# The second score product of both attentions: 64 rows of the array, or all 128

## The chip, the cores and the metric

The kernel runs as one program on one core of a Trainium2 chip. The metric is device time in microseconds (us) of one execution; lower is better. The core has a tensor engine (PE in the profile; its weight loads are listed apart, as PEld), a vector engine (DVE), a scalar engine (ACT), GpSimd (POOL), and DMA queues issued mostly from SyncE (SP).

## The reference

Two transformer blocks in a row, on 512 tokens of width 1024, in float32. Cut to what matters here:

```
# block 1: mixer = banded attention + pooling, gated; then a gated feed-forward with a short convolution
sc = einsum('bqhd,bkhd->bhqk', q_c, k_c) * scale + bias      # 8 heads of 64 features
p  = softmax(sc);  y = einsum('bhqk,bkhd->bqhd', p, v_c)

# block 2: gated delta rule (4 heads of 128) + differential attention (4 heads of 2 x 64)
sc = einsum("bqhcd,bkhcd->bhcqk", q_i, k) * scale            # c = 0, 1: two score maps for a head
p  = softmax(where(mask, sc, -inf));  p = p[:, :, 0] - lam * p[:, :, 1]
o  = einsum("bhqk,bkhe->bqhe", p, v)
```

In both attentions a score is a sum over 64 features, and causality leaves 128, 256, 384 or 512 keys for the four blocks of 128 queries.

## The kernel before

**Exactness.** Large products are made in float32r from operands that are split in two: a high part (the value copied to float32r) and a low part (what the copy lost, by a subtraction on the vector engine). A product is three passes: high by high, high by low, low by high. Each is a weight load of 128 columns and a matmul of up to 512 columns.

**Scores.** A score contracts over 64 features, half of the array's 128 rows. `stack_q` makes, for each of two heads (`j` = 0, 1), a tile of 128 partitions: the head's own 64 partitions hold the high part of the queries and the other 64 their low part. `stack_k` makes for each head a tile with the high part of the keys in both halves (`ka`, `kb`), and one tile `kl` with the low parts of both heads, each in its own half. `score` then needs two matmuls: the first over all 128 rows gives (q_hi + q_lo) k_hi, the second over the head's own 64 rows gives q_hi k_lo. The queries are the weights of both, the keys stream.

**Where they run.** Block 1 has 8 heads with 4 query blocks each: 32 scores (`attn_item`), their tiles stacked from an SBUF tile in `evac_qk`, once for each of four head pairs. Block 2 has 4 heads with 4 query blocks and 2 maps: 32 scores (`diff_item`), their tiles stacked from a PSUM bank in `to_heads`, once for each of four heads. So `stack_k` is called eight times and `score` 64 times.

**Order.** Each engine works through its instructions in the order in which they were issued. The class `Issue` keeps estimated times for every engine and tile; attention, convolution, delta rule and norms are background tasks (generators) which `step()` lets go on between two matmuls of the large products, when by these estimates their inputs are there. `Engine` wraps every engine, so that every instruction stands under one line (L230) in the profile. The estimate for a matmul does not depend on its rows:

```
            m, exact = ins[0].free_size(), ins[0].dtype != F32R
            t = (4 * max(n, m) if exact else max(n, m / 2) + 240 * self.exact) / 2400 + 0.003
```

**Buffers.** Tiles of 128 x 512 (`act(...)`) come from one pool of 75 buffers. Scores use two PSUM banks (`s`), transposes and small products three (`t`), large products three (`mm`). The weight stream (`w32`, `whi`, `wlo`) is fetched on the SP queue and split on ACT and DVE while the large products run.

**What consumes the result.** In block 1 the attention output (`ah`, `al`) is needed by the branch product that follows the gates. In block 2 the last product takes the heads in the order `HEADS`: the first six of them in all output tiles, then the last two, whose weights wait in tiles `wk`. Heads 6 and 7 are heads of the differential attention (`oh`, `ol`).

Of the kernel before, what the change touches and what calls it, by code (L numbers as in the profile page):

```python
# [29 lines left out]
# block 2's projections in order: a and z are feature-major tiles, the others two heads token-major  # L30
UNITS = ["a6", "a10", "a4", "a1", "a8", "a7", "a3", "a5", "a2", "a9", "q1", "v0", "a0", "q0",
         "k0", "z5", "a11", "k1", "z3", "z0", "z2", "z4", "z1", "z6", "z7", "v1"]
# heads in the order in which the last product takes them: the first of them in all tiles, then the others
# [7 lines left out]
# issue order: a task goes on when its last results are LEAD us away, unless an engine has SLACK us of work  # L41
# [23 lines left out]
def weight_order():  # L65
    """(array, piece, first column, end) in the order of use"""
    o = []

    def add(name, i=None, a=0, b=None):
        o.append((name, i, a, b))  # L70

    for hp in range(4):
        add("w_qk", 2 * hp)
        add("w_qk", 2 * hp + 1)
        if hp == 0:
            for i in range(4):
                add("w_v", i)
    add("w_pg")
    for i in range(4):
        add("w_u", i)  # L80
    for m in range(KD):
        add("w_g", 2 * m)
        add("w_g", 2 * m + 1)
        add("w_ap", m)
    for m in range(KD):
        add("w_o", m)
    for i in range(2 * MF):
        add("w_up", i)
    for m in range(KD):
        for a, b in ((0, 8), (8, 15), (15, 22)):  # L90
            add("w_dn", m, a * P, b * P)
    for u in UNITS:
        if u[0] in "az":
            add("w2_" + u[0], int(u[1:]))
        else:
            add("w2_" + u, 0)
            add("w2_" + u, 1)
    for m in range(KD):
        add("w_out", m)
    return o  # L100
# [5 lines left out]
class Issue:  # L106
    """Order of issue. Each engine works through its instructions in the order in which they are issued;
    the times that are kept here, in us, are estimates and decide that order alone."""
# [45 lines left out]
    def issue(self, e, op, outs, ins, func=None):  # L154
        self.count += 1
        lat = {"PE": 0.2, "V": 0.13, "A": 0.13, "G": 0.13}[e]
        start = max(self.free[e], self.ready(*ins) + lat)
        if e == "PE":
            start = max(start, self.now)
        # one engine at a time works on a PSUM bank  # L160
        held = [self.bank.setdefault(x.name, {}) for x in (*outs, *ins) if x.space == PSUM]
        for d in held:
            start = max([start] + [t + 0.05 for o, t in d.items() if o != e])
        if func in TABLES and TABLES[func] != self.table:
            self.table = TABLES[func]
            start += 1.28
        t = start + self.cost(e, op, outs, ins)
        for d in held:
            d[e] = t
        self.free[e] = t  # L170
        if e == "PE":
            self.now = t
        self.done(outs, t + (0.05 if e == "PE" else 0.0))
# [16 lines left out]
    def step(self):  # L190
        """tasks whose results have come go on; between two yields a task's work is issued together"""
        for task in list(self.tasks):
            if task[0] > self.now + LEAD:
                continue
            if not task[2] and max(self.free["V"], self.free["A"]) > self.now + SLACK:
                continue
            self.mark = task[3]
            r = next(task[1], "end")
            if r == "end":
                self.tasks.remove(task)  # L200
            else:
                task[0], task[3] = self.now if r == 0 else self.mark, self.mark
# [13 lines left out]
class Engine:  # L216
    """An engine whose instructions are counted by an Issue."""
# [18 lines left out]
def kernel(ctx, tc, aps, out, dbg=None):  # L236
# [13 lines left out]
    # PSUM banks: of each kind the time at which a bank's last readers are done  # L250
# [21 lines left out]
    # ---- background tasks: generators; "yield" waits for what was just issued, "yield 0" does not  # L272
# [4 lines left out]
    def move(dst, src):  # L277
        """a transfer within the chip's memories"""
# [3 lines left out]
    def grab_all(tag, n):  # L282
        """PSUM banks whose last readers are done"""
# [70 lines left out]
    # ---- weight stream: fetched three pieces ahead, split two ahead  # L354
# [16 lines left out]
    def split_next():  # L371
# [11 lines left out]
        elif key[0] == "w_out" and key[1] < NPART:  # L383
            # the first heads' weights pass through, the others' stay
# [26 lines left out]
    def weights(*key):  # L411
        """the next piece of the stream"""
        w = take(*key)
        advance()
        return w
# [6 lines left out]
    def wcol(w, k):  # L422
        """the weights of one k, of a piece that may wait in two halves"""
        return w[k // 4][:, k % 4 * P:(k % 4 + 1) * P] if isinstance(w, list) else w[:, k * P:(k + 1) * P]

    def mm(ps, w, x, start, stop):
        """a slice of a large product; while its operands are on their way other work goes on"""
# [34 lines left out]
    def copy(dst, src, scale=None):  # L462
        """on the engine that is free first"""
# [7 lines left out]
    def scale_rows(t, r):  # L471
        """t[p, c] *= r[p, c]"""
# [21 lines left out]
    def rstd(acc, col, tbs):  # L494
        """col[token] = 1 / rms and the same spread over the partitions"""
# [10 lines left out]
    class Seam:  # L506
        """x += rms_norm(f) and the next operand x * g split in two parts, one half of the tokens at a
        time: the norm of the first half runs under the products of the second."""
# [61 lines left out]
    def project_norm(wkeys, hi, lo, gname, seam, gnext):  # L570
        """f = W^T act in 8 output tiles; wkeys(m) lists each tile's pieces and their k ranges"""
# [27 lines left out]
    # ------------------------------------------------------------------ block 1: mixer  # L599
    # the first two products begin while their operands arrive  # L600
# [16 lines left out]
    # the tensor engine's clock rises while it works  # L617
# [60 lines left out]
    def attn_item(h, qb):  # L678
        """scores and softmax of (head, 128 queries)"""
# [40 lines left out]
    def attn_values():  # L720
        """transposed probabilities times values, (head pair, 128 keys) at a time"""
# [46 lines left out]
    def stack_q(src):  # L768
        """two heads of 64 features: for each its high part and, in the other half of the partitions, its low part"""
# [9 lines left out]
    def stack_k(src):  # L779
        """for each of two heads its high part in both halves, and their low parts"""  # L780
        a, b, lo = act("ka", F32R), act("kb", F32R), act("kl", F32R)
        parts = ((a, LOW, HIGH), (b, HIGH, LOW))
        for t, own, other in parts:
# [3 lines left out]
        for t, own, _ in parts:  # L787
            V.tensor_tensor(lo[own], src[own], t[own].bitcast(F32), op=ALU.subtract)
        return a, b, lo

    def score(ps, q, k, j, qs, n):
        """(q_hi + q_lo) k_hi, then q_hi k_lo"""
        own = (LOW, HIGH)[j]
        T.matmul(ps, q[j][:, qs], k[j][:, :n], start=True, stop=False)
        T.matmul(ps, q[j][own, qs], k[2][own, :n], start=False, stop=True)
# [56 lines left out]
    # pooling branch  # L852
# [44 lines left out]
    # gates, branch outputs, their mix  # L897
# [45 lines left out]
    # ------------------------------------------------------------------ block 1: feed-forward  # L943
# [37 lines left out]
    def seam_products(sn, keys, finish):  # L981
        """the first products after a seam, one half of the tokens at a time"""
# [72 lines left out]
    # inverses of the blocks of 16 x 16 go into zeros  # L1055
# [11 lines left out]
    # ------------------------------------------------------------------ block 2  # L1067
# [8 lines left out]
    def delta_gates():  # L1076
        """decays and write strengths, column c * 4 + h"""
# [74 lines left out]
    def gdn_pair(hs):  # L1152
        """two heads of the delta rule; chunks of 128 tokens. k, q and v carry a factor 2 from silu."""
# [12 lines left out]
        def decays():  # L1166
            """the chunks' running log decays on all partitions"""
# [41 lines left out]
        # the diagonal blocks of 64 x 64 of the chunks: [128, NT, 64], rows 0-63 one block, rows 64-127 the other  # L1209
        BLOCKS = ((LOW, LOW), (HIGH, HIGH))  # L1210
        halves = lambda t: t[:, :256].rearrange("p (c d) -> p c d", c=NT)
        # L passes through DRAM, where its diagonal blocks of 16, 32 and 64 lie at even distances
# [3 lines left out]
        def diag(t, n, row, w):  # L1216
            """of each of the diagonal blocks of n x n the rows from row on and w columns: [chunk, block, row, column]"""
# [38 lines left out]
        # off the inverse's path: values, keys and attention weights of the chunks  # L1256
# [46 lines left out]
        # inverse of I + L: 16 x 16 diagonal blocks by substitution, one block to a partition, then three merges  # L1303
# [31 lines left out]
        def inverse(i):  # L1335
            # T: transposed inverse of the blocks, D: the inverse, both compact
# [107 lines left out]
    def finish_head(o, ssq, idx, eps, nq=None):  # L1444
        """rms norm over the head, weight, silu(z), split: o is token-major [128, NT, 128]"""
# [29 lines left out]
    def tok_unit(nm, half_):  # L1475
        """token-major projection of two heads (256 columns): two [128, 2, 256] tiles of token blocks"""
# [26 lines left out]
    def v_unit():  # L1503
        """token-major values of the first two heads with the delta rule's b and a"""
# [21 lines left out]
    def rope_norm(nm, tok_):  # L1526
        """rms norm over 64 (its factor returned for q, applied for k) and rotation, in place"""
# [122 lines left out]
    # the residual waits in DRAM until the last product  # L1650
# [38 lines left out]
    def out_part(ps, w, a, b, cs=FULL, start=True, stop=True):  # L1689
        """the heads in places a to b"""  # L1690
# [20 lines left out]
    # the first heads in all tiles, then the last heads; three tiles wait in PSUM, the others' sums go to the residual  # L1711
# [29 lines left out]
def _pack(inputs):  # L1741
# [4 lines left out]
    def tiles(w):  # L1746
        """[K, N] -> [N/128, 128, K] pieces: one output tile's weights, k tiles side by side."""
# [3 lines left out]
    def tok_pieces(w, n):  # L1751
        """[1024, m*n] -> [m, 2, 128, 4*n]: token-major operands, half of k in each piece."""
# [94 lines left out]
```

## Time and profile before

| | us |
|---|---|
| median of 3 runs | 1041.13 |
| lowest and highest run | 1040.13, 1042.51 |
| span of the profiled execution | 1042.7 |
| PE busy in it | 1024.7 (98%) |
| PE weight loads busy | 849.2 (81%) |
| DVE busy | 684.9 (66%) |
| ACT busy | 499.5 (48%) |

The profiled execution is another one than the three timed; the page gives its span, from the first to the last instruction, and no time around it. Busy shares are means over the whole span. A matmul's end is modelled, so the durations of neighbouring matmuls overlap and PE looks busy also where it is not at its peak; what a matmul costs in a row of others is read from start to start. The granted TensorE clock is given as a share of its upper level, 2.4 GHz.

### The profile page before, as it was taken

Reading aid. Unit: us, or ns where it says so; the run is one execution under the profiler, and the core shown is the slowest. Engines: PE = TensorE matmul, PEld = TensorE weight load, DVE = VectorE, ACT = ScalarE, POOL = GpSimd, SP = SyncE. Lnnn points to the kernel's source line nnn. Section 1 sums busy time; section 2 is a strip of 40 time slices with the busy share of each in tenths; the row PEclk is TensorE's granted clock in tenths of the full one; section 3 lists DMA queues with packets and bytes.
Section 4 is the critical chain, followed back from the end, with each engine's and each line's share of the span. In section 5 each row is a group of like instructions: output and inputs, shape, how many; then the busy total and the mean of one; then the engine's idle time right before and its main releaser. Section 6 shows DMA issues by size and latency. Waiting matters only on the chain. (4 is left out here: it accounts for less than half of the span.)

```text
span 1042.7 us, 15097 instructions
## 1 busy us (share of the span) xinstructions
PE 1024.7 (98%) x5718; PEld 849.2 (81%) x5718; DVE 684.9 (66%) x1409; ACT 499.5 (48%) x1039; POOL 74.5 (7%) x146
## 2 busy tenths in 40 slices
PE   8999999999999999999999999999999989999998
PEld 7966678888888888888888888898899978887876
DVE  6576774444447897766776522359885687997873
ACT  6566643333244554434434421334456674667670
POOL 3000000000002200000001000004100450001001
PEclk9999999999999999999999999999999998999999
DMA  7321122332332133233233323330533530023212
GB/s 261 133 71 49 63 70 92 102 96 88 100 110 73 61 102 101 82 100 101 90 94 116 102 85 112 91 122 8 177 102 107 143 92 22 21 62 122 70 53 81
DMA packets 40345, 97.19 MB, mean 93 GB/s; under 512 B 12160, under 2 KB 16528, under 8 KB 40272
## 3 DMA queue, kind: packets, MB, share of 16 engines
q1 hardware_dynamic: 37392, 87.53, 26.7%
q0 software_dynamic: 2736, 8.66, 2.4%
q8 instruction: 45, 0.74, 0.3%
q14 instruction: 28, 0.23, 0.1%
q10 hardware_dynamic: 144, 0.03, 0.0%
HBM read 90.29 MB, written 5.91 MB: 92 GB/s over the span
## 5 line engine op out<-in xcount | busy, mean ns | idle before, releaser
L230 DVE TENSOR_TENSOR wlo<-w,whi 128x1024 fp32r<-128x1024 f32 (+4 forms) x153 | 180.5, 1185 | 63.7 <-ACT whi L230 63.7
L230 PE MATMUL mm<-nh,whi 128*128 128x512 f32 x448 | 177.5, 396 | 0.0
L230 PE MATMUL mm<-nl,whi 128*128 128x512 f32 x448 | 177.4, 396 | 0.0
L230 PE MATMUL mm<-nh,wlo 128*128 128x512 f32 x448 | 177.2, 395 | 0.0
L230 ACT ACTIVATE whi<-w 128x1024 fp32r<-128x1024 f32 (+4 forms) x153 | 154.9, 1017 | 40.3 <-DMA w<-w_dn 22.0
L230 PEld LDWEIGHTS mm<-nh,whi 128*128 128x128 f32 x448 | 84.3, 188 | 18.5 <-issue 0.8
L230 PEld LDWEIGHTS mm<-nh,wlo 128*128 128x128 f32 x448 | 84.3, 188 | 18.3 <-issue 0.2
L230 PEld LDWEIGHTS mm<-nl,whi 128*128 128x128 f32 x448 | 84.3, 188 | 18.0 <-issue 0.2
L230 PE MATMUL mm<-h,whi 128*128 128x512 f32 x208 | 83.5, 402 | 0.0
L230 PE MATMUL mm<-h,wlo 128*128 128x512 f32 x208 | 83.3, 400 | 0.0
L230 PE MATMUL mm<-l,whi 128*128 128x512 f32 x208 | 83.2, 400 | 0.0
L230 PE MATMUL mm<-gh,whi 128*128 128x512 f32 (+1 forms) x198 | 73.0, 369 | 0.0
L230 PE MATMUL mm<-gh,wlo 128*128 128x512 f32 (+1 forms) x198 | 72.8, 368 | 0.0
L230 PE MATMUL mm<-gl,whi 128*128 128x512 f32 (+1 forms) x198 | 72.8, 368 | 0.0
L230 ACT ACTIVATE y<-hu,par 128x512 f32<-128x512 f32 x40 | 32.6, 814 | 65.6 <-DVE hu L230 65.6
L230 DVE SCALAR_TENSOR_TENSOR y<-hu,par,y 128x511 f32<-128x511 f32 x80 | 59.8, 748 | 1.4
L230 POOL TENSOR_TENSOR acc<-acc,sq 128x256 f32<-128x256 f32 (+1 forms) x31 | 26.2, 846 | 426.0 <-ACT sq L230 425.9
L230 DVE TENSOR_TENSOR hu<-mm,nb 128x512 f32<-128x512 f32 x40 | 27.6, 690 | 42.2 <-PE mm L230 42.2
L230 PE MATMUL mm<-wlo,nh 128*128 128x256 f32 (+1 forms) x192 | 55.3, 288 | 0.0
L230 PE MATMUL mm<-whi,nl 128*128 128x256 f32 (+1 forms) x192 | 55.0, 287 | 0.0
L230 PE MATMUL mm<-whi,nh 128*128 128x256 f32 (+1 forms) x192 | 55.0, 286 | 0.0
L230 DVE TENSOR_TENSOR acc<-acc,sq 128x512 f32<-128x512 f32 (+1 forms) x21 | 14.3, 682 | 49.9 <-ACT sq L230 49.8
(343 smaller groups left out, 2203.2 us busy)
## 6 DMA issues: line engine op xcount, KB each, us to landing
w<-w_up SPq DMA_DIRECT2D x44, 512.0 KB, 3.5
w<-w_g SPq DMA_DIRECT2D x16, 512.0 KB, 3.5
w<-w_dn SPq DMA_DIRECT2D x16, 448.0 KB, 3.4
w<-w_a SPq DMA_DIRECT2D x12, 512.0 KB, 3.5
w<-w_ap SPq DMA_DIRECT2D x8, 512.0 KB, 3.5
w<-w_o SPq DMA_DIRECT2D x8, 512.0 KB, 3.4
w<-w_dn SPq DMA_DIRECT2D x8, 512.0 KB, 3.6
w<-w_z SPq DMA_DIRECT2D x8, 512.0 KB, 3.8
```

The lines of the kernel that those rows point to most:

```text
L230: return f(*args, **kw)
```

## The change

`stack_k` now makes four tiles: `ka` and `kb` as before, and `la` and `lb`, which hold a head's low part of the keys in both partition halves. `score`'s second matmul takes all 128 rows of the query tile and of `la` or `lb`. It computes (q_hi + q_lo) k_lo: the term q_lo k_lo, left out before, comes in. For each call of `stack_k` there are four subtractions on DVE in the place of two, and four buffers in the place of three. Numbers and sizes of matmuls stay. The rest of the diff takes out comments and docstrings.

```
     def stack_k(src):
-        a, b, lo = act("ka", F32R), act("kb", F32R), act("kl", F32R)
-        parts = ((a, LOW, HIGH), (b, HIGH, LOW))
-        for t, own, other in parts:
+        a, b, la, lb = act("ka", F32R), act("kb", F32R), act("la", F32R), act("lb", F32R)
+        parts = ((a, la, LOW, HIGH), (b, lb, HIGH, LOW))
+        for t, _, own, other in parts:
             A.activation(t[own], src[own], AF.Copy)
             A.activation(t[other], src[own], AF.Copy)
         yield
-        for t, own, _ in parts:
+        for t, lo, own, other in parts:
             V.tensor_tensor(lo[own], src[own], t[own].bitcast(F32), op=ALU.subtract)
-        return a, b, lo
+            V.tensor_tensor(lo[other], src[own], t[own].bitcast(F32), op=ALU.subtract)
+        return a, b, la, lb
 
     def score(ps, q, k, j, qs, n):
-        own = (LOW, HIGH)[j]
         T.matmul(ps, q[j][:, qs], k[j][:, :n], start=True, stop=False)
-        T.matmul(ps, q[j][own, qs], k[2][own, :n], start=False, stop=True)
+        T.matmul(ps, q[j][:, qs], k[2 + j][:, :n], start=False, stop=True)
```

## Rows read from the trace of the kernel before

**Rows 1.** The page, part 1: busy us, share of the span, instructions.
```profile
PE 1024.7 (98%) x5718; PEld 849.2 (81%) x5718; DVE 684.9 (66%) x1409; ACT 499.5 (48%) x1039; POOL 74.5 (7%) x146
```

**Rows 2.** Busy time by stretch: from:to, length, engines (instructions), clock, DMA share, GB/s.
```profile
44.00:122.00 78.00, 78.00 (x343) 49.89 (x341) 52.74 (x152) 48.77 (x118) 1.61 (x3) 1.00 0.19 65
880.00:946.00 66.00, 65.11 (x431) 53.21 (x430) 61.03 (x190) 44.45 (x136) 0.00 (x0) 1.00 0.15 47
946.00:1020.00 74.00, 73.90 (x415) 59.95 (x414) 57.10 (x190) 51.46 (x151) 4.31 (x8) 1.00 0.25 79
```

**Rows 3.** Timeline of PE, block 1: start us, duration us, instruction, rows*columns, operand.
```profile
118.65 0.34 PE L230 MATMUL s<-kb,qb 128*128 128x384 f32 x1
118.92 0.43 PE L230 MATMUL s<-kl,qb 64*128 64x384 f32 x1
119.29 0.50 PE L230 MATMUL s<-kb,qb 128*128 128x512 f32 x1
119.72 0.50 PE L230 MATMUL s<-kl,qb 64*128 64x512 f32 x1
120.15 0.50 PE L230 MATMUL mm<-l,whi 128*128 128x512 f32 x1
120.48 0.40 PE L230 MATMUL mm<-h,wlo 128*128 128x512 f32 x1
120.72 0.39 PE L230 MATMUL mm<-h,whi 128*128 128x512 f32 x1
```

**Rows 4.** Timeline of the weight loads (PEld) of the same stretch.
```profile
118.42 0.19 PEld L230 LDWEIGHTS s<-kb,qb 128*128 128x128 f32 x1
118.92 0.18 PEld L230 LDWEIGHTS s<-kl,qb 64*128 64x128 f32 x1 [0.31 <-issue]
```

**Rows 5.** Timeline of PE, block 1, a score over 256 keys.
```profile
52.54 0.28 PE L230 MATMUL s<-kb,qb 128*128 128x256 f32 x1
52.75 0.38 PE L230 MATMUL s<-kl,qb 64*128 64x256 f32 x1
53.06 0.50 PE L230 MATMUL mm<-l,whi 128*128 128x512 f32 x1
53.40 0.40 PE L230 MATMUL mm<-h,wlo 128*128 128x512 f32 x1
```

**Rows 6.** Timeline of PE, block 2, two scores over 128 keys.
```profile
927.89 0.22 PE L230 MATMUL s<-ka,qa 128*128 128x128 f32 x1
928.04 0.33 PE L230 MATMUL s<-kl,qa 64*128 64x128 f32 x1
...
928.81 0.49 PE L230 MATMUL mm<-nl,whi 128*128 128x512 f32 x1
929.14 0.39 PE L230 MATMUL mm<-nh,wlo 128*128 128x512 f32 x1
```

**Rows 7.** The chain that ended last, merged: start us, us, engine, tile, count.
```profile
885.60 0.69 DVE kl L230
...
888.91 0.49 PE t L230 x2
...
962.62 5.95 PE mm L230 x49
```

**Rows 8.** Instructions of tile kl: durations ns (min/median/max), first to last start, forms.
```profile
L230 PE MATMUL s<-kl,qa x32: 323/410/502, 45.3 to 998.4; 64*128 64x128 f32 x8, 64*128 64x256 f32 x8, 64*128 64x384 f32 x8, 64*128 64x512 f32 x8
L230 PE MATMUL s<-kl,qb x32: 322/410/498, 51.7 to 999.3; 64*128 64x128 f32 x8, 64*128 64x256 f32 x8, 64*128 64x384 f32 x8, 64*128 64x512 f32 x8
L230 DVE TENSOR_TENSOR kl<-qk,kb x4: 689/689/689, 35.9 to 110.6; 64x512 fp32r<-64x512 f32 x4
L230 DVE TENSOR_TENSOR kl<-t,kb x4: 694/694/695, 885.6 to 955.1; 64x512 fp32r<-64x512 f32 x4
```

**Rows 9.** Instructions of tile al, the attention's result in block 1.
```profile
L230 PEld LDWEIGHTS mm<-al,whi x32: 187/188/192, 158.2 to 276.1; 128*128 128x128 f32 x32
...
L230 DVE TENSOR_TENSOR al<-mm,ah x4: 683/688/692, 82.4 to 142.3; 128x512 fp32r<-128x512 f32 x4
```

**Rows 10.** Instructions of tile ol, the heads' results in block 2.
```profile
L230 PEld LDWEIGHTS mm<-ol,wk x16: 186/188/192, 1028.6 to 1038.7; 128*128 128x128 f32 x16
...
L230 DVE TENSOR_TENSOR ol<-z,oh x8: 679/684/685, 936.6 to 1018.6; 128x512 fp32r<-128x512 f32 x8
```

## The prediction, as it was made before the run

> **What bounds the kernel.** I read the page first. Over the whole span PE is busy 98% and the next engine, DVE, 66% [rows 1]. A modelled busy share doesn't prove that PE is at its limit, so I went on to the stretches with scores. In block 1's attention (44 to 122 us) PE has no idle time and DVE is busy 52.74 of 78 us, 68%. In block 2's attention PE is as full, but DVE is busy 61.03 of 66 us from 880 to 946 (92%) and 57.10 of 74 from 946 to 1020 (77%); the clock is at its upper level, 2.4 GHz, in all three [rows 2]. The chain of waits agrees: it runs over DVE until the first low parts of block 2's keys at 885.60, and from 888.91 on over PE almost without a break [rows 7]. So time taken from PE should come off the end, with one place to watch, DVE between 880 and 946.
>
> Then the timeline of PE, from start to start. In a run of large products a 512-column matmul takes 120.72 - 120.48 = 0.24 us. Around a score the steps are longer: 0.27 and 0.37 us for 384 keys, 0.43 and 0.43 for 512, and the large product behind them still takes 0.33 [rows 3]. The weight loads say why. The load of a 128-row score product starts 0.23 us ahead of its matmul (118.42 against 118.65). The load of the 64-row product starts together with its matmul, at 118.92, after 0.31 us in which no load ran [rows 4]. Each time the array goes from 128 rows to 64, or back, the next load is not made ahead.
>
> **The change on PE.** It removes both kinds of switch, 64 pairs in all: 16 each of 128, 256, 384 and 512 keys [rows 8]. I take it that a full-height second product is pipelined like the full-height products beside it; the rows show that for passes that accumulate in one bank too.
>
> - 384 and 512 keys: from 118.65 to 120.48 two scores and a large product take 1.83 us [rows 3]. At the undisturbed rate, 0.24 us for 512 columns and three quarters, 0.18, for 384, they take 2 x 0.18 + 3 x 0.24 = 1.08. The two pairs save 0.75, or 0.375 each.
> - 256 keys: one score and the large product take 53.40 - 52.54 = 0.86 us [rows 5]. Undisturbed 256-column products take 5.95 / 49 = 0.121 each [rows 7], so 2 x 0.12 + 0.24 = 0.48 is left. Saved: 0.38.
> - 128 keys: two scores and the large product take 929.14 - 927.89 = 1.25 us [rows 6]. No row has undisturbed 128-column matmuls in float32r. Each needs a weight load of the size that the 256-column ones need, so 0.12 is the upper bound; a quarter of 0.24, or 0.06, is the lower. I take 0.12, since its load is the same one: 1.25 - 4 x 0.12 - 0.24 = 0.53, or 0.265 a pair. The lower bound gives 0.12 more a pair, 1.9 us over 16.
>
> Sum: 16 x (0.375 + 0.375 + 0.38 + 0.265) = 22.3 us, up to 24.2; half of it, 11.2, in each block. That the whole of it lies on the path of the end is what the next part has to cut.
>
> The Trainium skill, page "TensorE: Matmul & The Clock Gate", section "Part 3: Packing small matmuls", states that a weight load overlaps matmuls in flight only when their row groups differ. By that rule the full-height second product would wait for its load just as the 64-row one does, and the sum on PE would be 0 and not 22.3; this case's trace disagrees, since full-height loads start 0.23 us ahead of their matmuls among other full-height products [rows 4].
>
> **The change on DVE.** Each of eight `stack_k` calls gets two more subtractions of 0.69 us [rows 8]: 16 x 0.69 = 11.0 us, 5.5 in each block. What covers them:
>
> - Block 1. The first call's sources are ready by 36 us, nine us before the first score at 45.3 [rows 8], so its 1.4 us are hidden. The other three add 4.1 to 52.74 us of DVE; if PE's 11.2 us come off, that is 56.9 of 66.8, 85%. The attention's last result starts on DVE at 142.3 and is wanted from 158.2 [rows 9], 15 us of room. Even if the chain there got no faster and 4.1 later, the product would wait less than a microsecond once PE comes 11.2 earlier. I charge 1 us, and 0 to 4 for the range.
> - Block 2, 880 to 946. Two calls add 2.8 us, and 61.03 + 2.8 = 63.8 of work can't be done in less; PE wants 66 less some 5.6, or 60.4 [rows 2]. The stretch can shrink by 2.2 at most where all that PE does needs DVE. But much of PE's work there is projections that need nothing of the attention, and the order lets them go ahead. The first call lies on the chain [rows 7], so its 1.4 us count in full. I charge 2.5, with bounds of 1.4 and 5.6.
> - Block 2, 946 to 1020. Two more calls: 57.10 + 2.8 = 59.9 in 74 - 5.6 = 68.4 us, 88%. The last head's low part starts at 1018.6 (0.68 long) and is first wanted at 1028.6, nine us later [rows 10], which takes up what the attention loses against PE. Nothing charged, up to 2.8.
>
> Behind the added subtractions in DVE's queue stand score evacuations, delta-rule steps and weight splits. PE waits for all three in the end, and that wait is what I charged. ACT's work is unchanged, 48.77 of 78 us in block 1 [rows 2]. In block 2 the source is a PSUM bank, held 1.4 us longer a call; it is one of three. The one buffer more per call, of 75, I cost at nothing, covered by the 15 and nine us of room; without that cover it would add to the waits charged. DMA is at 0.25 or less in these stretches [rows 2].
>
> Net: 22.3 - 1 - 2.5 = 18.8 us. Against the profiled execution that is 1042.7 - 18.8 = 1023.9; the median of the runs lies 1.6 below that span, so 1022.3.
>
> **Rivals.** *DVE becomes the bound.* PE gets faster, and the attentions follow DVE. For it: 92% of DVE from 880 to 946, and 5.5 us added where it is fullest. Against it: 15 and nine us of room, and projections to fill with. Block 1 then keeps 11.2 less 1 to 4, block 2 between 0 and 11.2 - 5.6 - 2.8 = 2.8. Total 7 to 13, so 1028 to 1034; call it 1031.
>
> *The second product keeps its price,* so the change does nothing on PE. The extra rows cost no time, but the load is late for another reason than the switch, say that it loads the same query tile as the product before. Then only DVE's additions are left, 0 to 5.5 us behind the cover: 1041 to 1045. Against it: the first product of a following pair also pays, 0.43 against 0.24, and so does the large product behind, 0.33 [rows 3]; neither shares that trait. The same page's section on LDWEIGHTS says that a load's time depends on columns, not rows. That agrees with 0.18 and 0.19 us [rows 4], and leaves this rival where it was.
>
> *The last head comes too late (slower).* Its low part is done at 1019.3. With PE 18.8 earlier the last product would want it at 1009.8; the chain, too, gets faster by what PE gave it. To end slower than before, the chain must slip more than 9.3 us behind its old time. The additions in block 2 are 5.5; it takes every one of them on the chain and 4 us more of queueing. At twice 5.5 the end is 1041.1 + 11 - 9.3 = 1043. From 9.3 on it decides.
>
> **How the numbers follow.** Forecast 0.68, DVE bound 0.23, price kept 0.06, last head late 0.03. The predicted time is the forecast's, 1022.3. Its own range is 24.2 saved less 1.4 charged, to 22.3 less 7 (the upper charges, not all at once): 1018 to 1026. The range for 8 in 10 reaches from 1017.5 (24.2 less almost nothing) to 1032, which takes in some two thirds of the DVE rival. A difference under 0.2%, 2 us, is about what a measurement of this kernel can't tell from none. Faster is 0.68 + 0.23, and 0.01 of the last rival: 0.92. The price-kept case splits evenly, same 0.03 and slower 0.03; with the last rival's other 0.02, slower is 0.05.
>
> **What would show it.** In the changed profile the load of the second score product starts ahead of its matmul; steps of 0.24, 0.18 and 0.12 us; 0.24 for the large product behind. DVE 11 us busier in all, about 95% from 880 on. PE idle grows by 2 to 5 us, on waits for DVE between 880 and 960. If loads still start with their matmuls, the second rival holds. If the steps are short but PE's waits for DVE sum to over 8 us, the first does. A wait ahead of the first product with `wk` means the third.

## The result, and the profile after

| | before | changed |
|---|---|---|
| median of four runs, us | 1041.79 | 1028.74 |
| lowest and highest, us | 1040.13, 1042.51 | 1027.33, 1031.49 |
| span of the profiled execution, us | 1042.7 | 1026.7 |

The ratio is 0.9865 (95%: 0.9837 to 0.9893), so the change is worth 14.1 us with 11.1 to 17.0 as its interval; the medians are 13.1 apart. The forecast was 18.8. The spans of the two profiled executions differ by 16.0; single runs of one kernel differ by some microseconds (last section), so the size is taken from the ratios and the place from the traces.

Part 1 of the page after, against [rows 1]:

```profile
PE 1004.9 (98%) x5718; PEld 844.8 (82%) x5718; DVE 693.5 (68%) x1429; ACT 496.6 (48%) x1032; POOL 74.4 (7%) x146
```

PE is busy 19.8 us less with as many instructions. It is not busy for 1026.7 - 1004.9 = 21.8 us, and was for 1042.7 - 1024.7 = 18.0: 3.8 more. DVE has 20 instructions more, 16 of them the subtractions. The other four, three copies of `scr` and one multiplication of `do` in the place of four, came from ACT, which has seven fewer: the helpers `copy` and `scale_rows` choose between ACT and DVE by the booked times. What is called the order below includes these few choices.

Timeline of PE in block 1, with the columns of [rows 3]:

```profile
107.85 0.43 PE L230 MATMUL s<-kb,qb 128*128 128x384 f32 x1
108.11 0.34 PE L230 MATMUL s<-lb,qb 128*128 128x384 f32 x1
108.29 0.39 PE L230 MATMUL mm<-l,whi 128*128 128x512 f32 x1
...
109.12 0.48 PE L230 MATMUL s<-kb,qb 128*128 128x512 f32 x1
109.43 0.40 PE L230 MATMUL s<-lb,qb 128*128 128x512 f32 x1
109.67 0.39 PE L230 MATMUL mm<-l,whi 128*128 128x512 f32 x1
109.90 0.39 PE L230 MATMUL mm<-h,wlo 128*128 128x512 f32 x1
```

and the weight load of the second product at 109.43:

```profile
109.20 0.19 PEld L230 LDWEIGHTS s<-lb,qb 128*128 128x128 f32 x1
```

From the second product to the next instruction it is 0.18 us for 384 keys and 0.24 for 512, the large product behind takes 0.23, and the load starts 0.23 us ahead of its matmul. Before, these steps were 0.37, 0.43 and 0.33 [rows 3], and the load started with its matmul [rows 4]. (The first products here stand behind an exact transpose and step 0.26 and 0.31.) In block 2, 128 keys:

```profile
928.41 0.31 PE L230 MATMUL s<-ka,qa 128*128 128x128 f32 x1
928.55 0.27 PE L230 MATMUL s<-la,qa 128*128 128x128 f32 x1
928.67 0.27 PE L230 MATMUL s<-kb,qb 128*128 128x128 f32 x1
928.78 0.27 PE L230 MATMUL s<-lb,qb 128*128 128x128 f32 x1
928.89 0.45 PE L230 MATMUL mm<-nl,whi 128*128 128x512 f32 x1
```

Three steps are 0.12, 0.11 and 0.11 us; four products take 0.48, where they took 0.92 [rows 6].

Tiles `la`, `al` and `ol`, with the columns of [rows 8 to 10]:

```profile
L230 DVE TENSOR_TENSOR la<-qk,ka x8: 673/684/685, 34.7 to 100.6; 64x512 fp32r<-64x512 f32 x8
L230 DVE TENSOR_TENSOR la<-t,ka x8: 671/678/686, 873.2 to 936.1; 64x512 fp32r<-64x512 f32 x8
```
```profile
L230 PEld LDWEIGHTS mm<-al,whi x32: 187/188/192, 147.5 to 265.4; 128*128 128x128 f32 x32
...
L230 DVE TENSOR_TENSOR al<-mm,ah x4: 683/688/692, 77.7 to 132.1; 128x512 fp32r<-128x512 f32 x4
```
```profile
L230 PEld LDWEIGHTS mm<-ol,wk x16: 186/188/192, 1012.7 to 1022.7; 128*128 128x128 f32 x16
...
L230 DVE TENSOR_TENSOR ol<-z,oh x8: 683/685/694, 932.5 to 996.4; 128x512 fp32r<-128x512 f32 x8
```

A subtraction costs what it was said to, 0.67 to 0.69 us. Block 1's result is wanted 158.2 - 147.5 = 10.7 us earlier, nearly the 11.2 of the array alone, and lies ready 14.7 us ahead. The last low part of `ol` starts 22.2 us earlier than in [rows 10] and is done (996.4 + 0.7) 15.6 us ahead of the first load of `wk` weights.

So the gain of block 1 came whole, and what is missing was lost in block 2. Where, the windows of the second attention say (columns of [rows 2]):

```profile
869.00:945.00 76.00, 75.14 (x514) 64.06 (x514) 72.67 (x217) 48.81 (x148) 4.30 (x8) 1.00 0.18 57
945.00:986.00 41.00, 36.76 (x240) 31.67 (x240) 37.75 (x147) 36.16 (x114) 0.00 (x0) 1.00 0.20 67
```

To 945 PE has under a microsecond without work, though DVE is busy 96%. From 945 to 986 PE lacks 4.2 us, where the kernel before had 0.1 in all of 946 to 1020 [rows 2]. Timeline of PE in that stretch (in brackets: idle before, and what ended it):

```profile
958.33 0.50 PE L230 MATMUL mm<-ol,whi 128*128 128x512 f32 x1 [0.79 <-DVE ol L230]
958.67 0.39 PE L230 MATMUL mm<-oh,wlo 128*128 128x512 f32 x1
960.23 0.94 PE L230 MATMUL t<-vtok,et 128*128 128x128 f32 x6 [1.17 <-ACT et L230]
...
962.53 1.16 PE L230 MATMUL t<-vtok,et 128*128 128x128 f32 x8 [0.21 <-ACT et L230]
...
968.99 0.27 PE L230 MATMUL s<-lb,qb 128*128 128x128 f32 x1
970.47 0.55 PE L230 MATMUL t<-cst,e 128*128 128x128 f32 x3 [1.21 <-DVE e L230]
...
975.10 0.30 PE L230 MATMUL t<-cst,e 128*128 128x128 f32 x1 [0.40 <-DVE e L230]
```

What stands between the scores here are pieces of the last product (`oh`, `ol`). The last projection product starts at 955.6, so behind it there is no projection any more, and where a probability (`e`, `et`) isn't ready, PE has nothing else. The waits of PE from 945 to 986 (sum, times, longest):

```profile
PE t L230 <- DVE e L230: 1.6, 2, 1.2
PE t L230 <- ACT et L230: 1.4, 2, 1.2
PE mm L230 <- DVE ol L230: 0.8, 1, 0.8
PE s L230 <- DVE mx L230: 0.3, 2, 0.2
```

That is 4.1 us. Two theories remained. *Load:* the added subtractions keep DVE from the evacuations and the softmax. *Order:* `Issue` books the added subtractions as DVE time, so it lets attention and large products go on at other moments, and this order leaves PE short of other work. A third, that the array's saving was smaller than thought, had to be ruled out.

### The profile page after: what moved, and what is told of

The parts are those of the page before. It is cut to its first block, busy times and chain, and to the rows that moved or that the text cites. A ratio compares the mean times of both kernels' runs of the same rounds, so it can differ in the third digit from the quotient of the medians.

```text
span 1026.7 us, 15112 instructions
## 1 busy us (share of the span) xinstructions
PE 1004.9 (98%) x5718; PEld 844.8 (82%) x5718; DVE 693.5 (68%) x1429; ACT 496.6 (48%) x1032; POOL 74.4 (7%) x146
## 4 chain that ended last, share of the span: by engine, by line
PE 79%; DVE 13%; DMA 3%; ACT 2%; issue 1%; POOL 1%; SPq 0%; DVEq 0%; ACTq 0%
PE mm L230 71%; PE t L230 5%; PE s L230 3%; DVE nl L230 2%; DVE x L230 2%; DVE wlo L230 1%; DVE f L230 1%; DVE e L230 1%; DVE rsq_t L230 1%; DMA w<-w_up 1%; DMA T<-dx 1%; POOL xt L230 1%; DMA w<-w_qk 1%; DVE acc L230 1%; POOL cb L230 1%
## 5 line engine op out<-in xcount | busy, mean ns | idle before, releaser
L230 ACT ACTIVATE whi<-w 128x1024 fp32r<-128x1024 f32 (+4 forms) x153 | 154.8, 1018 | 42.7 <-DMA w<-w_dn 22.1
L230 PEld LDWEIGHTS mm<-nh,whi 128*128 128x128 f32 x448 | 84.3, 188 | 18.1 <-issue 0.4
```

The costliest lines, as they stand in the source:

```text
L230: return f(*args, **kw)
```

## The experiments

All ratios are to the kernel before, measured beside them on the same chip; the microseconds are those of the ratio on its median in the same set. The code is cut to the lines that differ from the changed kernel (for `grouped`, from the kernel before).

**First set (kernel before 1043.38): one block alone, and one half of the change alone.**

`block1_only` and `block2_only` keep the old `stack_k` and the 64-row second product in the other block:

```
-            kT[hp] = yield from stack_k(t)        # block2_only
+            kT[hp] = yield from stack_k_old(t)
-        yield from to_heads(kt, k_, stack_k)      # block1_only
+        yield from to_heads(kt, k_, stack_k_old)
```

> Full-height second product and four key tiles in block 1 alone; block 2 as before. My theory (the array's saving is whole in block 1, and what is missing is lost in block 2 to DVE): 11 us faster than before, 1030 to 1032, and the large products behind block 1 start 10.7 to 11 us earlier than before, as in the changed kernel. Rival (the two blocks share the loss, since the vector work of block 1 also delays the end): 6 to 9 us faster.

> The change in block 2 alone. My theory (DVE is short there, PE runs out of projections in the second half of the differential attention): 2 to 6 us faster than before, 1036 to 1040, with PE waits for DVE or ACT of 3 to 5 us in the last 100 us. Rival (the saving on the array is whole and the missing part of the changed kernel was an accident of its order): 9 to 11 us faster, 1031 to 1033.

`dve_only` makes `la` and `lb` in both halves, but the second product reads 64 rows:

```
+        own = (LOW, HIGH)[j]
-        T.matmul(ps, q[j][:, qs], k[2 + j][:, :n], start=False, stop=True)
+        T.matmul(ps, q[j][own, qs], k[2 + j][own, :n], start=False, stop=True)
```

> The four subtractions and four tiles in both blocks, but the second product still uses 64 rows. My theory: the vector work is covered where PE is slow: nothing in block 1, 0 to 3 us slower through block 2, 1041 to 1045. Rival (the subtractions cost their own length): 6 to 11 us slower. If it comes out faster, the order alone moves the time by that much.

`zero_half` keeps the full-height product and takes the DVE work away: zeros from GpSimd stand in the other half. The term q_lo k_lo is left out again, as in the kernel before:

```
         yield
+        for _, lo, _, other in parts:             # ahead of this yield
+            G.memset(lo[other].bitcast(F32), 0.0)
-            V.tensor_tensor(lo[other], src[own], t[own].bitcast(F32), op=ALU.subtract)
```

> All 128 rows, but the other half of the low tile is filled with zeros by GpSimd and not by two subtractions on DVE, so that the array's saving stands without the 11 us on DVE; the term q_lo k_lo is left out as in the kernel before. My theory (DVE's load in block 2 takes the rest): 3 to 6 us faster than the changed kernel, 1022 to 1026. Rival (the rest is lost to the order or to slower steps of PE in block 2, not to DVE's load): as the changed kernel, 1027 to 1031.

| | median us | ratio (95%) | against before, us |
|---|---|---|---|
| block1_only | 1033.56 | 0.9922 (0.9901 to 0.9944) | 8.1 faster |
| block2_only | 1039.63 | 0.9981 (0.9964 to 0.9998) | 2.0 faster |
| dve_only | 1046.43 | 1.0047 (1.0027 to 1.0067) | 4.9 slower |
| zero_half | 1020.6 | 0.9802 (0.9778 to 0.9827) | 20.7 faster |

The forecast had 11.2 - 1 = 10.2 in block 1 and 11.2 - 2.5 = 8.7 in block 2. Block 2 gives 2.0 (0.2 to 3.8): the gap is there, and from 880 to 1000 its trace has the waits of the changed kernel, 1.6 us for `e`, 1.4 for `et` and 1.0 for `ol`. Block 1 gives 8.1 (5.8 to 10.3), less than the 11 expected and in the 6 to 9 of the rival, that block 1's vector work also delays the end. Its trace doesn't settle this: the first `al` load comes 10.7 us earlier, as in the changed kernel, and the first `wk` load 9.5 earlier (1019.1), but in that execution the clock also fell once more (last section). `zero_half` gives 20.7 (18.1 to 23.2), its median is below the 1022 to 1026 that were expected, and the interval holds the forecast 22.3; so the array's saving was not too small.

`dve_only` costs more than expected, and more than the waits of PE that its trace shows. In the traces its PE, ACT and DVE have the sequence of the changed kernel, so it holds load and order together, beside the slower 64-row products. In it a stretch at half the clock stands behind the starved part, and its nine runs had a mean granted clock of 0.9938 where the kernel before had 0.9972, an estimated 3 us by the rate of the last section; so its 4.9 (2.8 to 7.0) are not all load and order.

`zero_half` changes two things: DVE's work is less, and, as DVE is booked the old time, PE, DVE and ACT get exactly the order of the kernel before (in the traces all three have the same sequence). The second set took these apart.

**Second set (kernel before 1043.23): load and order apart.**

`same_order` makes the added subtractions, but unknown to `Issue`; PE and ACT then have the order of the kernel before:

```
-            V.tensor_tensor(lo[other], src[own], t[own].bitcast(F32), op=ALU.subtract)
+            nc.vector.tensor_tensor(lo[other], src[own], t[own].bitcast(F32), op=ALU.subtract)
```

> The changed kernel, but the added subtractions are hidden from the planner, so that PE, ACT and the rest of DVE work in the order of the kernel before, with 16 more instructions in DVE's queue. Theory A (the missing 5 to 7 us go to DVE's load in block 2): as the changed kernel or a little slower, 1027 to 1033. Theory B (they go to the order that the planner makes when it counts these subtractions): 1019 to 1023, as with zeros.

`zero_after_order` has the zeros and no added subtraction (again without q_lo k_lo), but books the subtraction; PE and ACT then have the order of the changed kernel:

```
+            nc.gpsimd.memset(lo[other].bitcast(F32), 0.0)    # ahead of the yield
-            V.tensor_tensor(lo[other], src[own], t[own].bitcast(F32), op=ALU.subtract)
+            iss.issue("V", "tensor_tensor", [lo[other]], [src[own], t[own]])
```

> Zeros by GpSimd in the other half of the low tile (q_lo k_lo left out, no subtractions added), but the planner is told of the two subtractions, so that PE, ACT and DVE work in the order of the changed kernel. Theory A (DVE's load): 1019 to 1024, as zeros in the old order. Theory B (the order): as the changed kernel, 1027 to 1031. Between the two, both count.

`act_copy` has ACT copy the low part to the other half:

```
-            V.tensor_tensor(lo[other], src[own], t[own].bitcast(F32), op=ALU.subtract)
+        yield
+        for _, lo, own, other in parts:
+            A.activation(lo[other], lo[own].bitcast(F32), AF.Copy)
```

> All 128 rows, and the low part is carried to the other half by a copy on ACT after the subtraction, not by a second subtraction on DVE: 16 more instructions of 0.6 us on an engine that is busy 48%, and one step more before the first score. Theory A (DVE's load): 2 to 6 us faster than the changed kernel, 1022 to 1027. Theory B (the order): anything from 1020 to 1031, as the planner's order falls out.

`grouped` is the kernel before, with block 2's products in another sequence, so that the two of 64 rows stand together:

```
-            score(ps[c][:, :n], q, k, c, slice(qb * P, n), n)
+            T.matmul(ps[c][:, :n], q[c][:, qs], k[c][:, :n], start=True, stop=False)
+        for c in range(2):
+            own = (LOW, HIGH)[c]
+            T.matmul(ps[c][:, :n], q[c][own, qs], k[2][own, :n], start=False, stop=True)
```

> The kernel before, with one edit in block 2: for the two maps of a head the two 128-row products come first and the two 64-row products behind them, so that the array goes to 64 rows and back once for two scores and not twice. If the price is that of the switch: some 0.38 us less for each of 16 groups, 4 to 6 us faster than before, no vector work added. If the price is the 64-row product's own (its load comes late whatever stands beside it): 0 to 1 us.

| | median us | ratio (95%) | faster by, us |
|---|---|---|---|
| same_order | 1026.18 | 0.9839 (0.9817 to 0.9860) | 16.8 |
| zero_after_order | 1025.59 | 0.9829 (0.9807 to 0.9851) | 17.8 |
| act_copy | 1025.6 | 0.9835 (0.9815 to 0.9854) | 17.2 |
| grouped | 1035.23 | 0.9929 (0.9911 to 0.9947) | 7.4 |

By their medians both theories hold a part: taking away the order alone or the load alone leaves the time between the changed kernel and `zero_half`. `act_copy` does no better than either; it has an order of its own, and in its trace the clock fell a second time (last section).

`grouped` bears on the price of the switch. A group has half as many switches; timeline of PE with 256 keys, and its loads:

```profile
932.77 0.36 PE L230 MATMUL s<-ka,qa 128*128 128x256 f32 x1
932.97 0.28 PE L230 MATMUL s<-kb,qb 128*128 128x256 f32 x1
933.18 0.38 PE L230 MATMUL s<-kl,qa 64*128 64x256 f32 x1
933.18 0.39 PE L230 MATMUL s<-kl,qb 64*128 64x256 f32 x1
933.50 0.50 PE L230 MATMUL mm<-nl,whi 128*128 128x512 f32 x1
```
```profile
933.18 0.18 PEld L230 LDWEIGHTS s<-kl,qa 64*128 64x128 f32 x1
933.18 0.18 PEld L230 LDWEIGHTS s<-kl,qb 64*128 64x128 f32 x1
```

The switch is still there, 0.21 and 0.32 us around it, but the two 64-row products, in opposite halves of the array, start together, loads too, so one of them costs no step at all. It is so in all 16 groups of the trace. That is more than the halved switches that I had counted. The Trainium skill, page "TensorEngine Tiling (Array Packing)", section "Key Properties", says that a change of tiling mode drains TensorE and that different tiles run independently; these rows agree with both.

**Third set (kernel before 1041.93): all four corners on one chip.** `after_2x2` is the changed kernel itself, `same_order_2x2` and `zero_after_order_2x2` are the kernels of the second set, and `zero_2x2` is `zero_half` with its fills unbooked too:

```
+            nc.gpsimd.memset(lo[other].bitcast(F32), 0.0)    # ahead of the yield
-            V.tensor_tensor(lo[other], src[own], t[own].bitcast(F32), op=ALU.subtract)
```

> The changed kernel again, on the same chip as the next three, so that DVE's load (added subtractions or zeros) and the order (the changed kernel's or the one before) can be told apart in one call. If both count and add up: 1028 to 1031, 7 to 9 us above zeros in the old order.

> Added subtractions on DVE, order of the kernel before. If both count: 3 to 6 us above zeros in the old order (load), 1 to 4 below the changed kernel (order). If DVE's load alone counts: as the changed kernel, within 1.5 us. If the order alone: as zeros in the old order, within 1.5 us.

> Zeros by GpSimd (q_lo k_lo left out), order of the changed kernel. If both count: 2 to 5 us below the changed kernel, 1 to 5 above zeros in the old order. If DVE's load alone: as zeros in the old order. If the order alone: as the changed kernel.

> Zeros by GpSimd (q_lo k_lo left out), order of the kernel before. The fastest of the four, 20 to 23 us faster than the kernel before, if the array's saving of 22 us is whole once DVE and the order are left alone.

| | old order | new order |
|---|---|---|
| no added subtractions | `zero_2x2` 1019.6; 0.9782 (0.9757 to 0.9806) | `zero_after_order_2x2` 1025.58; 0.9833 (0.9809 to 0.9858) |
| 16 subtractions more | `same_order_2x2` 1025.14; 0.9833 (0.9810 to 0.9856) | `after_2x2` 1029.09; 0.9871 (0.9847 to 0.9895) |

On 1041.93 us the array's saving is 22.7 us (20.2 to 25.3). The load costs 5.3 in the old order and 4.0 in the new; the order costs 5.3 without the load and 4.0 with it. Each of these differences is uncertain by about 3.5 us, but all four have the same sign, and so they have with the earlier sets: with the mean ratios of both measurements of each corner (0.9792, 0.9831, 0.9836, 0.9868) they are 4.6, 3.9, 4.1 and 3.3. Together load and order take back 9.3 us (7.9 by the means). The profiled executions, two of each corner and all at a mean granted clock of 0.997 or 0.998, repeat within 0.7 us. Their spans are 1017.7 and 1017.7 with neither (`zero_half`, `zero_2x2`), 1024.2 and 1023.5 with the load alone, 1024.2 and 1024.6 with the order alone, 1026.7 and 1026.0 with both. Read by these, either one alone costs some 6 to 7 us and the other adds 1.4 to 2.5: that the two simply add up is not shown.

The waits of PE in the second attention (868 to 986, 865 to 986 in the last) show the place. `zero_after_order_2x2`:

```profile
PE t L230 <- DVE e L230: 1.6, 2, 1.2
PE t L230 <- ACT et L230: 0.9, 2, 0.7
PE t L230 <- DVE Dc L230: 0.6, 1, 0.6
PE s L230 <- DVE mx L230: 0.3, 2, 0.2
```

`same_order_2x2`:

```profile
PE t L230 <- DVE T L230: 1.3, 1, 1.3
PE t L230 <- DVE e L230: 0.8, 1, 0.8
PE t L230 <- DVE Dc L230: 0.6, 1, 0.6
PE t L230 <- DVE lb L789: 0.5, 2, 0.3
```

`zero_2x2`:

```profile
PE t L230 <- DVE Dc L230: 0.6, 1, 0.6
PE t L230 <- DVE T L230: 0.4, 1, 0.4
PE t L230 <- DVE e L230: 0.2, 1, 0.2
```

With the new order PE waits for `e`, `et` and `mx` as in the changed kernel, though no subtraction was added. With the load in the old order it waits for other things: for `T` of the delta rule, and for the subtraction itself (`lb`). With neither, 1.2 us are left. How the order does it can be counted in the timelines of PE, from the start of the last 512-column projection product to the start of the last score product. Behind that projection product every kernel has 96 products of 256 columns, the last projection, first and nearly in one piece; pieces of the last product come after them:

```
                       from     to      us    last projection  last product  score products  small ones (t)
before                 962.4    999.3   36.9        96              47             32             35
after                  941.0    977.0   36.0        96              15             36             76
zero_after_order_2x2   940.6    974.9   34.2        96              15             36             76
same_order_2x2         948.9    980.4   31.4        96              47             32             35
zero_2x2               943.1    974.5   31.4        96              47             32             35
```

The new order has four score products and some 40 transposes and value products more here, and 32 pieces of the last product (7.5 us at 0.235) fewer. Behind the last projection, 32 score products are still to come in either order; the old one has 47 pieces to put between them, the new one 15. The other 32 run behind the attention instead. Why `Issue` holds them back was not followed in its booked times. Both ends are nearly the same in the changed kernel and in `zero_2x2` (977.0 and 974.5), but `zero_2x2` is by then 7.5 us of large products further. In its row of windows PE has no gap (to be read beside that of 945 to 986):

```profile
941.00:977.00 36.00, 36.00 (x246) 32.92 (x245) 32.37 (x121) 29.38 (x89) 0.00 (x0) 1.00 0.28 93
```

`zero_2x2` is the best version of the study, 22.7 us under the kernel before, 9.3 under the changed one. Its zeros cost 16 fills of 0.52 us on GpSimd, which is busy 8% there. Part 1 of its page:

```profile
PE 1000.8 (98%) x5718; PEld 844.2 (83%) x5718; DVE 682.3 (67%) x1409; ACT 498.3 (49%) x1039; POOL 82.6 (8%) x162
```

Of the 9.0 us between its span (1017.7) and that of the changed kernel, 4.9 are time in which PE isn't busy (16.9 against 21.8), and 4.1 are longer busy time for as many matmuls (1000.8 against 1004.9). Products behind an exact transpose step longer, as seen in block 1, and the new order mixes more transposes with the scores; that these make up the 4.1 is not shown.

## Why the prediction was right, and where its size was off

The mechanism and the sign were right, and the time lies in the range, 6.4 us over the value given. It does not lie in the forecast's own 1018 to 1026: the range reached up to 1032 to take in part of the first rival. That the time fell inside was the work of this margin, not of the sum.

**The saving on PE: right.** The steps are 0.24, 0.18 and 0.11 to 0.12, the load starts ahead, and the kernels without the added DVE work save 20.7 and 22.7 us, where 22.3 to 24.2 were said. The rule of the Trainium skill, page "TensorE: Matmul & The Clock Gate", section "Part 3: Packing small matmuls", that a load overlaps matmuls in flight only when their row groups differ, is again not what the trace shows: among full-height products the load at 109.20 is 0.23 us ahead of its matmul. The second rival, the price kept, falls with it.

**Block 1's charge of 1 us: right within the error.** The first `al` load comes 10.7 us earlier in the changed kernel, and 11.9 earlier (146.3) in `zero_2x2`: the load and the order cost 1.2 there (0.6 by `after_2x2`, with 146.9). The 15 us of room held.

**Block 2's charge of 2.5 us: the step that failed.** The three charges together were 3.5 us; the runs make them 8 to 9. Two things were wrong in it. First, the working counted DVE's extra work once, as time on a chain; by the medians it costs 4 to 5 us over the kernel in either order, for 11 us of added work by the sum of its records. Second, there is no term for the order. The sentence "much of PE's work there is projections that need nothing of the attention, and the order lets them go ahead" took the filler as given. But the order depends on DVE's booked time, the added subtractions move it, and the filler runs out: the last projection product starts at 955.6, 32 score products are still to come, and 15 pieces of the last product stand among them where there were 47. That is another 3 to 5 us by the medians. For 946 to 1020, matched now by 945 to 986, nothing was charged since the result at its end had nine us of room. The room was there, 15.6 us even, but what waited was PE in the middle, for probabilities, with no other product to make. The buffer more for each call, costed at nothing, shows no cost: `zero_2x2` takes it too and has the whole saving.

**The signs to look for.** DVE is 8.6 us busier, not 11. The 16 records of 0.68 sum to 10.9, but records of neighbouring instructions overlap and count once in busy time: with the order held, the subtractions add 9.5 (693.5 against 684.0 in `zero_after_order_2x2`) and 9.8 (692.1 in `same_order_2x2` against 682.3 in `zero_2x2`). It is busy 96% from 869 to 945, as was said. PE's idle time grows by 3.8 us, in the 2 to 5 that were said, but the waits lie between 957 and 976, most of them behind the 880 to 960 that were named, and 1.4 us are waits for ACT. So the right idle time came from a wrong split, which was luck: against `zero_2x2` the idle time is 4.9 us longer, and nearly as much of the loss is longer busy time, for which there was no term.

**The first rival, DVE as the bound,** gives 1028 to 1034, and the time is just inside. The sign named for it, over 8 us of waits for DVE, is absent: from 870 to 986 they sum to 3.5. And `zero_after_order_2x2`, without the added work, waits at the same places. So this rival has the time and only half of the reason. **The third rival** is absent: no wait ahead of `wk`.

What stays open: the split of the 8 to 9 us into load and order is known to about 3 us, the two overlap in the profiled executions, and part of each may be the clock (below).

## What to carry to other kernels

A matmul on fewer rows than its neighbours was not cheaper here but dearer; count what the switch costs on both sides, and fill the other rows with whatever costs nothing, zeros from an idle engine before anything that the busy engine has to make. Where the order of issue follows booked times, an added instruction on one engine changes the order on all, so time the change in the old order as well before its cost is put down to the instruction. A stretch with a full PE is safe only as long as other products are left: count the filler up to the end of the stretch.

## What the runs showed of the hardware

**Two 64-row products in opposite halves run together** when they are issued behind each other (`grouped`, both at 933.18, loads too): the group costs one step for both.

**The scatter of the runs goes with the clock.** In the traces the granted clock falls to 1.2 GHz for some microseconds after PE has waited for block 2's start (3.5 us for one tile in the kernel before), and in `dve_only` once more, behind the starved part of the attention. Windows of the kernel before, and of `dve_only`:

```profile
860.00:865.00 5.00, 4.99 (x45) 4.86 (x45) 0.68 (x1) 1.29 (x3) 0.00 (x0) 0.50 0.01 3
```
```profile
980.00:986.00 6.00, 5.16 (x24) 3.27 (x23) 5.48 (x30) 4.67 (x15) 0.00 (x0) 1.00 0.00 1
987.00:996.00 9.00, 9.00 (x31) 6.77 (x31) 4.99 (x18) 5.54 (x22) 0.00 (x0) 0.50 0.00 1
```

The clock is 0.50 in the first and the last, 1.2 GHz. In `act_copy` it fell a second time too (0.50 from 969 to 971, behind 8 us in which PE was busy 6.16), and in `block1_only` around 327 to 331 (0.58, behind 7 us with PE busy 6.02). In the changed kernel it stayed at 1.00 from 945 to 986, though PE lacked 4.2 of the 41 us. The runs of a kernel go with it: `dve_only` took 1043.53 us at a mean granted clock of 0.997 and 1050.34 at 0.989, the kernel before, in the same set, 1039.05 at 1.000 and 1045.16 at 0.995. By that, about a microsecond for 0.001. `after_2x2` had 0.9948 in the mean of its four runs and `zero_2x2` 0.9970, so some 2 of the 9.3 us between them may be clock; one run of each at 0.997, 1027.10 and 1019.42, are 7.7 apart. So gaps in PE's work may cost more than their own length.
